# Five queue orders in a two-layer streaming encoder: sample bias sign, gate tiles, output weight loads, low-rank turns and sample rotary queries

## The chip, the cores and the metric

The kernel runs on one core of one Trainium2 chip. The metric is the device time of one launch in microseconds (us). Five engines of the core work side by side, each through its own list of instructions: PE does matmuls and transposes, DVE, ACT and POOL do elementwise work, and SP issues the DMA transfers. An engine waits where the next instruction of its list needs something that another engine, or a transfer, has not yet delivered.

## The reference, cut to what matters

The reference is one inference step of two transformer-like layers for 1024 prompt rows and 8 x 16 sample rows, the latter with caches of 512 earlier rows. Each layer projects x with one matrix and runs three groups of attention heads, each gated, whose results go through one output matrix and a layer norm:

```python
h = einsum('btd,de->bte', x, w_in)      # c_q, c_kv, k_rope, gates, fox q/k/v, log-forget, memory q
q   = _rms_norm(c_q, q_norm_g) @ w_uq;  q[..., 128:] = _rope(q[..., 128:], pos)
lat = _rms_norm(c_kv, kv_norm_g);       kr = _rope(k_rope, pos)
o_mla = _attend(q, [lat @ w_uk, kr], lat @ w_uv, chunk_causal=True)
o_fox = _attend(fq, fk, fv, logits += cq[t] - ck[s])   # cq, ck: running sums of log-forget
o_mem = softmax(mq @ mem_k) @ mem_v
mixed = concat([o_mla * silu(g_mla), o_fox * silu(g_fox), o_mem * silu(g_mem)])
y = layer_norm(ALPHA * x + mixed @ w_out)
```

All arithmetic is in float32 and the outputs also hold the new cache rows (latents, rotary keys, fox keys and values, log-forget).

## The kernel before, in words

A float32 product is made of three matmuls on operands split into a high and a low part (lines 192, 193 and 194: high by high, low by high or high by low). The split itself is a copy on ACT and a subtraction on DVE (L176, L177), and for weights a copy on ACT (L183) and a subtraction on POOL (L186). Work is tiled by 128 rows: tiles 0 to 7 are the prompt, tile 8 is all samples.

The two layers run the same stages one after the other, layer 0 up to about 755 us and layer 1 after it: memory gates (`w_ge`) and memory attention, with the fox gates (`w_gf`) and the sample memory attention woven in; forget sums and fox attention with its gates (`w_gm`); the low-rank projections; the queries, `qlat`, `qrope` and `s_qrope`; the latent (MLA) attention by head, with the sample attention woven in; and the output projection with the layer norm.

The order on each engine is not written by hand. The Python code emits the instructions through generators that are interleaved by small constants, and a scheduler with a timeline model then reorders them within their dependences and writes one list for each engine. Tiles come from pools with a fixed number of slots: a new tile waits until the readers of the slot's former tile are done. The pools that matter here are `w` (8 slots, weights and some large tiles), `u` (25 slots), `st` (4), `th` (3, shared by the tanh of the gates, by `o64` attention outputs that are stored to `md`, and by rotary temporaries named `rt`), and in PSUM `pss` (3), `psx` (2), `pst` (2) and `pso` (1).

The five places:

- **Sample bias sign** (`s_fox`, L1113, and `scores`, L1132 and L1134). The running forget sums of the sample rows are loaded into `scq` by four small DMAs, DVE multiplies them by -1 (L1113), and POOL later adds them to the key sums. The prompt's fox attention starts at the same time: ACT copies the transposed prompt sums to a tile `st`, SP stores it to DRAM (`ckd`), loads it back spread over all partitions (`ckb`, 512 KB), and POOL makes the bias tiles `pf` from it (L585, and L586 for the causal edge). DVE adds a score tile and its bias (L432). The queries `qf` are written by ACT and DVE (L351, L352).
- **Gate tiles** (`gates`, L374 and L376). ACT writes tanh(x/2) into a tile of the `th` pool, and DVE makes (tanh + 1) x from it into a tile of the `st` pool, which SP stores to `gd`.
- **Output weights** (`wout`). When head 3 of the MLA attention begins, all eight 512 KB row blocks of `w_out` are loaded (`raw`, from the `w` pool) and split into `woh` and `wol` in one piece of code.
- **Low-rank turns** (`lowrank`). Two passes go over the nine tiles, in the order 8, 0, 1, ... 7, the first with the weights `lr0` and the second with `lr1`, each 128 x 1224 in two halves. The second pass normalises each tile (`norm`; POOL scales the query part at L721) and rotates its key (`rope`, six DVE instructions L664 to L669, and a POOL copy at L725). After tile 0 the sample tile is transposed on PE, after tile 3 and after tile 7 four prompt tiles each (`turn`, through PE L201, then split). The tile `kr` comes from the `w` pool after the `lr1` weights.
- **Sample rotary queries** (`s_qrope`). One matmul, a rotation (`qturn`) and two transposes run in one go behind head 0 of the query projection.

## Time and profile before

| | us |
|---|---|
| median of 3 runs | 1462.06 (1461.39 to 1464.06) |
| the profiled execution, its own time | 1465.12 |
| its span | 1463.3 |
| PE busy | 1408.9 (96%) |
| DVE, ACT, POOL busy | 765.9, 617.5, 505.6 |

The page gives busy times and the chain of work that ended last. The view of waits lists, for one engine, what it waited for: the waiting group, the releasing group, the total in us, the number of waits, and the longest. The timeline lists instructions with start, duration and, in brackets, the idle time of the engine just before and what ended it. The windows view gives for a stretch the busy time and the number of instructions of each engine, and the clock that PE was granted (PEclk, 1.00 is full speed).

### The profile page before, as it was taken

How to read it: one execution, taken by the hardware profiler on the slowest of the kernel's cores; microseconds unless marked ns; L12 is line 12 of the kernel's file. 1: busy time of each engine (PE TensorE's matmuls, PEld its weight loads, DVE VectorE, ACT ScalarE, POOL GpSimd, SP SyncE). 2: the span in 40 equal slices, each digit the busy share in tenths (PEclk: the TensorE clock that was granted, in tenths of full speed). 3: DMA queues.
4: the chain of work that ended last, by engine and by line, in shares of the span. 5: the costliest groups of instructions: out<-in, count | busy, mean ns of one | idle time of the engine just before them, and what ended most of it. 6: DMA issues, size and time to landing. Idle time of an engine off the chain costs nothing.

```text
span 1463.3 us, 27842 instructions
## 1 busy us (share of the span) xinstructions
PE 1408.9 (96%) x10222; PEld 1262.3 (86%) x10222; DVE 765.9 (52%) x1961; ACT 617.5 (42%) x1624; POOL 505.6 (35%) x738
## 2 busy tenths in 40 slices
PE   7999999999999999999999999999999999998997
PEld 6998979988988788888899988899899887787886
DVE  6236445254345665656663374542633556556564
ACT  6345345355154444622233453543532544455100
POOL 0234145354263221611322242534534532235021
PEclk9999999999999999999999999999999999999999
DMA  7223332445354332363541234233543533433531
GB/s 281 90 76 94 118 104 82 127 128 152 94 169 132 120 115 77 115 220 101 183 167 54 85 98 146 69 95 111 160 135 112 171 114 113 125 116 119 172 127 72
DMA packets 142343, 180.63 MB, mean 123 GB/s; under 512 B 32384, under 2 KB 99776, under 8 KB 142208
## 3 DMA queue, kind: packets, MB, share of 16 engines
q1 hardware_dynamic: 142208, 178.86, 38.7%
q8 instruction: 81, 1.33, 0.4%
q14 instruction: 54, 0.44, 0.1%
HBM read 138.69 MB, written 40.12 MB: 122 GB/s over the span
## 4 chain that ended last, share of the span: by engine, by line
PE 80%; DMA 6%; DVE 5%; ACT 3%; POOL 2%; issue 2%; SPq 1%; POOLq 0%; DVEq 0%; ACTq 0%
PE pss L192 13%; PE pss L194 13%; PE pss L193 13%; PE pss L197 9%; PE pso L197 7%; PE pst L201 6%; PE psx L197 6%; PE psx L192 4%; PE psx L194 4%; PE psx L193 4%; SPq L164 1%; PE psx L201 1%; DMA scq<-cumd 1%; DMA raw<-in_w_out_dram 1%; DMA x<-in_x_t_dram 1%
## 5 line engine op out<-in xcount | busy, mean ns | idle before, releaser
L186 POOL TENSOR_TENSOR wl<-raw,wh 128x1024 fp32r<-128x1024 f32 (+3 forms) x40 | 101.5, 2541 | 232.5 <-ACT wh L183 124.1
L177 DVE TENSOR_TENSOR ptw<-pst,ptw 128x512 fp32r<-128x512 f32 (+1 forms) x192 | 121.8, 642 | 80.5 <-ACT ptw L176 78.2
L176 ACT CAST ptw<-pst 128x512 fp32r<-128x512 f32 (+1 forms) x192 | 103.1, 550 | 97.8 <-PE pst L201 78.2
L192 PE MATMUL psx<-xh,wh 128*128 128x256 f32 x384 | 110.6, 288 | 9.6 <-ACT wh L183 6.6
L192 PE MATMUL pss<-wh,xh 128*128 128x306 f32 (+1 forms) x384 | 118.4, 309 | 0.0
L193 PE MATMUL pss<-wl,xh 128*128 128x306 f32 (+1 forms) x384 | 117.8, 307 | 0.0
L194 PE MATMUL pss<-wh,xl 128*128 128x306 f32 (+1 forms) x384 | 117.5, 307 | 0.0
L192 PE MATMUL pss<-woh,msh 128*128 128x512 f32 x288 | 114.0, 396 | 0.5 <-ACT msh L1231 0.5
L194 PE MATMUL pss<-woh,msl 128*128 128x512 f32 x288 | 114.0, 397 | 0.1
L193 PE MATMUL pss<-wol,msh 128*128 128x512 f32 x288 | 113.5, 394 | 0.0
L192 PE MATMUL pss<-xh,wh 128*128 128x256 f32 x384 | 111.4, 290 | 0.0
L193 PE MATMUL psx<-xl,wh 128*128 128x256 f32 x384 | 109.6, 286 | 0.0
L193 PE MATMUL pss<-xl,wh 128*128 128x256 f32 x384 | 109.6, 285 | 0.0
L194 PE MATMUL pss<-xh,wl 128*128 128x256 f32 x384 | 109.4, 285 | 0.0
L194 PE MATMUL psx<-xh,wl 128*128 128x256 f32 x384 | 108.7, 284 | 0.0
L397 POOL TENSOR_SCALAR pa<-pa,col 128x128 f32<-128x128 f32 (+3 forms) x64 | 47.9, 757 | 139.5 <-DVE col L396 94.4
L192 PEld LDWEIGHTS psx<-xh,wh 128*128 128x128 f32 x384 | 73.9, 192 | 10.6 <-ACT wh L183 6.6
L197 PE MATMUL pso<-ptw,vh 128*128 128x256 f32 (+1 forms) x336 | 73.6, 295 | 5.8 <-ACT ptw L176 4.0
L192 PEld LDWEIGHTS pss<-wh,xh 128*128 128x128 f32 x384 | 72.4, 189 | 3.9 <-issue 2.9
L192 PEld LDWEIGHTS pss<-xh,wh 128*128 128x128 f32 x384 | 73.7, 192 | 1.5 <-DVE col L432 0.6
L420 ACT ACTIVATE pa<-pss,col 128x512 f32<-128x512 f32 (+3 forms) x96 | 55.4, 584 | 44.5 <-DVE col L418 27.5
L193 PEld LDWEIGHTS pss<-xl,wh 128*128 128x128 f32 x384 | 73.8, 192 | 0.3
(365 smaller groups left out, 4205.9 us busy)
## 6 DMA issues: line engine op xcount, KB each, us to landing
gd<-gg SPq DMA_DIRECT2D x64, 128.0 KB
kT<-in_fox_kt_dram SPq DMA_DIRECT2D x32, 256.0 KB
vraw<-in_fox_v_dram SPq DMA_DIRECT2D x32, 256.0 KB
kT<-in_mla_kt_dram SPq DMA_DIRECT2D x32, 256.0 KB
vraw<-in_mla_v_dram SPq DMA_DIRECT2D x32, 256.0 KB
raw<-in_w_out_dram SPq DMA_DIRECT2D x16, 512.0 KB
g<-md SPq DMA_DIRECT2D x16, 512.0 KB
raw<-in_w_lr_dram SPq DMA_DIRECT2D x8, 612.0 KB
```

Source lines behind the costliest of these rows:

```text
L164: self.nc.sync.dma_start(dst, src)
L176: nc.scalar.copy(hi, ps)
L177: nc.vector.tensor_tensor(lo, ps, self.f(hi), op=ALU.subtract)
L186: (self.nc.vector if dve else self.nc.gpsimd).tensor_tensor(lo, raw, self.f(hi), op=ALU.subtract)
L192: self.nc.tensor.matmul(ps, ah, bh, start=first and x == 0, stop=False)
L193: self.nc.tensor.matmul(ps, ah, bl, start=False, stop=False)
L194: self.nc.tensor.matmul(ps, al, bh, start=False, stop=last and x == n - 1)
L197: self.nc.tensor.matmul(ps, lhsT, rhs, start=start, stop=stop)
L201: self.nc.tensor.transpose(out, in_, self.ident[:k, :k])
L397: self.nc.gpsimd.tensor_scalar(p, p, rs, 1.0, op0=ALU.mult, op1=ALU.mult)
L420: nc.scalar.activation(p[:, a:b], pss[x][:, :b - a], AF.Exp, bias=nmx[:, one], accum_out=sm[:, x:x + 1])
```

## The change

It edits five places, in both layers.

1. The multiplication by -1 goes, and POOL subtracts `scq` where it added it.
2. The gates write tanh and product into the same `st` tile; no `th` tile is used.
3. `wout` becomes a generator of five steps that loads four, two and two blocks and splits the pairs a step later; it is stepped from the third step of head 2 on and at each step of head 3.
4. In `lowrank`, the keys of all nine tiles are rotated by six DVE instructions and one POOL copy after tile 3 of the first pass; `kr` is therefore taken from the `w` pool before the `lr1` weights. The turns of the sample tile and of tiles 0 to 3 come one tile later, and before the last turns stand two steps of `qlat`.
5. `s_qrope` yields between its rotation and its transposes, which now follow head 1.

```diff
-                t = self.th([P, 256])
-                nc.scalar.activation(t, ps, AF.Tanh, scale=0.5)
                 g = self.st([P, 256], name="gg")
-                nc.vector.scalar_tensor_tensor(g, t, 1.0, ps, op0=ALU.add, op1=ALU.mult)
+                nc.scalar.activation(g, ps, AF.Tanh, scale=0.5)
+                nc.vector.scalar_tensor_tensor(g, g, 1.0, ps, op0=ALU.add, op1=ALU.mult)
...
+            if i == 3:
+                kr = self.w([P, 9, 2, 64], name="kr")
+                x1, x2 = early[:, :, 32:64], early[:, :, 64:96]
+                t = self.pw([P, 2, 9, 32], name="rt")
+                k1, k2 = kr[:, :, 0, 0:32], kr[:, :, 0, 32:64]
+                nc.vector.tensor_tensor(t[:, 0], x2, self.sin, op=ALU.mult)
...
+                nc.gpsimd.tensor_copy(kr[:, :, 1, :], kr[:, :, 0, :])
         W = self.wprep(self.i["w_lr1"][l])
...
-        kr = self.w([P, 9, 2, 64], name="kr")
...
-            self.rope(kr[:, i, 0:1, :], early[:, i, 32:96].unsqueeze(1), i, 1, nc.vector)
-            nc.gpsimd.tensor_copy(kr[:, i, 1, :], kr[:, i, 0, :])
...
+            if i == 1:
+                turn8()
+                yield
+            if i == TURN[0] + 1:
+                turns(0)
+                yield
+        self.wq0 = self.wmla("w_uqn", l, 0, 3)
+        more()
+        turns(1)
+        yield
...
         q = self.qturn(ps, 8, self.st)
+        yield
         pt = self.pso() if QPO else self.pst()
...
-        nc.vector.tensor_scalar(cq, cq, -1.0, None, op0=ALU.mult)
...
-            nc.gpsimd.tensor_scalar(pr[:, 0:512], ck, 1.0, cq[:, p:p + 1], op0=ALU.mult, op1=ALU.add)
+            nc.gpsimd.tensor_scalar(pr[:, 0:512], ck, 1.0, cq[:, p:p + 1], op0=ALU.mult, op1=ALU.subtract)
...
-    def wout(self, l):
-        WO = []
-        for e in range(8):
-            raw = self.w([P, D], name="raw")
-            self.load(raw, self.i["w_out"][l, e * P:(e + 1) * P, :])
-            hi = self.u([P, D], F32R, "woh")
-            lo = self.u([P, D], F32R, "wol")
-            self.wsplit(hi, lo, raw)
-            WO.append((hi, lo))
-        return WO
+    def wout(self, l, WO):
+        raws = []
+        for step in range(5):
+            if step:
+                for raw in raws[2 * step - 2:2 * step]:
+                    hi = self.u([P, D], F32R, "woh")
+                    lo = self.u([P, D], F32R, "wol")
+                    self.wsplit(hi, lo, raw)
+                    WO.append((hi, lo))
+            for e in range(*((0, 4), (4, 6), (6, 8), (8, 8), (8, 8))[step]):
+                raw = self.w([P, D], name="raw")
+                self.load(raw, self.i["w_out"][l, e * P:(e + 1) * P, :])
+                raws.append(raw)
+            yield
...
-                if h == 3:
-                    WO.extend(self.wout(l))
+                    if h == 3 or h == 2 and x == 2:
+                        next(wo)
```

The scheduler sees other code, so all engines' lists shift, not only at the five places. Three places show it. Line numbers of the new kernel are one higher than those of the old one up to the rotation code, and others behind it.

**SP and DVE where fox attention starts in layer 0.** SP before; `ckd` is the store of the prompt sums, `ckb` their load, `md` stores of memory attention outputs:

```order
L164 DMA raw_3353<-in_w_kv_dram 128x1208 [waits Pool_49]
L167 DMA md_134<-th_2100 64x256 [waits DMAHW5_49,DVE_49]
L167 DMA gd_127<-gg_2132 128x256 [waits DMAHW6_49]
L167 DMA gtd_142<-ggt_2138 128x256 [waits DMAHW7_49,Activation_49]
L167 DMA gd_128<-gg_2168 128x256 [waits DMAHW0_49,DVE_49]
L167 DMA ckd_140<-st_2212 32x128 [waits DMAHW1_49,Activation_49]
L167 DMA cumd_141<-spr_2235 32x528 [waits DMAHW2_49]
L164 DMA raw_3355<-in_w_kv_dram 128x1208 [waits DMAHW3_49,Pool_49]
L164 DMA g_2733<-gd_127 64x256 [waits DMAHW6_49,DMAHW4_49]
L164 DMA ckb_2397<-ckd_140 128x1024 [waits DMAHW5_49,DMAHW1_49]
L164 DMA ckb_2842<-ckd_140 128x1024
```

The same place now:

```order
L168 DMA md_132<-th_2001 64x256 [waits DMAHW1_49,DVE_49]
L165 DMA g_2082<-gd_130 64x256 [waits DMAHW2_49]
L168 DMA gd_128<-gg_2149 128x256 [waits DMAHW3_49,DVE_49]
L168 DMA ckd_140<-st_2194 32x128 [waits DMAHW4_49,Activation_49]
L168 DMA cumd_141<-spr_2217 32x528 [waits DMAHW5_49]
L168 DMA md_133<-th_2064 64x256 [waits DMAHW6_49,DVE_49]
L165 DMA ckb_2379<-ckd_140 128x1024 [waits DMAHW7_49,DMAHW4_49]
L165 DMA g_2593<-gd_127 64x256 [waits DMAHW0_49]
L165 DMA kT_2463<-in_mem_kt_dram 128x512 [waits DMAHW1_49,PE_49]
L165 DMA vraw_2547<-in_mem_v_dram 128x512 [waits DMAHW2_49,PE_49]
L165 DMA ckb_2820<-ckd_140 128x1024 [waits DMAHW3_49]
L168 DMA md_134<-th_2084 64x256 [waits DVE_49]
```

The store of `ckd` and the first load of `ckb` now stand ahead of the last `md` store, which was ahead of them, and the second `ckb` load has left the first. On DVE the row of L1113 is gone. Before, DVE read:

```order
L352 SCALAR_TENSOR_TENSOR qf_2245<-pss_2334,qf_2245 64x256 [waits Activation_49]
L1113 TENSOR_SCALAR scq_4928<-scq_4928 128x4 [waits DMAHW2_49,DMAHW1_49,DMAHW7_49,DMAHW0_49,DVE_49]
L352 SCALAR_TENSOR_TENSOR qf_2246<-pss_2334,qf_2246 64x256 [waits Activation_49]
L432 ISA pf_2399,col_2410<-pss_2404,pf_2399 128x512 [waits PE_49,Pool_49]
L432 ISA col_2410 128x1
```

On PE the transpose of the prompt sums stands 113 rows ahead of the first fox score now, and stood 129 rows ahead before. Also on PE, in the stage before this one, the fox gates now lie in blocks between the transposes and value products of memory attention, where these products stood next to each other before and most gates after them.

**PE where the second low-rank pass starts in layer 0.** `wh` and `wl` are the split weights, `xsh` and `xh` the sample and prompt rows. Before, tile 7 of the first pass was followed by a whole half of the next weights:

```order
L193 MATMUL pss_5222<-wl_4840,xh_504 128x306
L194 MATMUL pss_5222<-wh_4839,xl_505 128x306
L192 MATMUL pss_5275<-wh_5262,xsh_572 128x306 [waits Activation_49]
L193 MATMUL pss_5275<-wl_5263,xsh_572 128x306 [waits Pool_49]
L194 MATMUL pss_5275<-wh_5262,xsl_573 128x306
L192 MATMUL pss_5275<-wh_5262,xsh_572 128x306
L193 MATMUL pss_5275<-wl_5263,xsh_572 128x306
```

Now the first matmul of three tiles comes first, and then the one that waits for POOL:

```order
L194 MATMUL pss_5194<-wl_4804,xh_500 128x306
L195 MATMUL pss_5194<-wh_4803,xl_501 128x306
L193 MATMUL pss_5246<-wh_5234,xsh_566 128x306 [waits Activation_49]
L193 MATMUL pss_5309<-wh_5234,xh_106 128x306 [waits Activation_49]
L193 MATMUL pss_5355<-wh_5234,xh_106 128x306 [waits Activation_49]
L194 MATMUL pss_5246<-wl_5235,xsh_566 128x306 [waits Pool_49]
L195 MATMUL pss_5246<-wh_5234,xsl_567 128x306
```

The low part `wl_5235` is written into a slot of the `w` pool that tile 7 of the first pass reads until 12 matmuls before its end; in the old list only the low part of the other half (`wl_5267`) had to wait for such a slot, and PE had 28 matmuls to do before it.

**ACT in the last head of the MLA attention, layer 0.** `woh` is the high part of an output weight block, `ptw` the high part of a transposed probability tile, `pa` the exponentials. Before:

```order
L183 CAST woh_7912<-raw_7910 128x1024 [waits DMAHW2_49]
L183 CAST woh_7918<-raw_7916 128x1024 [waits DMAHW4_49]
L183 CAST woh_7924<-raw_7922 128x1024 [waits DMAHW5_49,PE_49]
L176 CAST ptw_7859<-pst_7855 128x384 [waits PE_49,Activation_49]
L420 ACTIVATE pa_7829,col_7831<-pss_7816,col_7830 128x512 [waits DVE_49,Activation_49,Pool_49]
L420 ACTIVATE pa_7829,col_7831<-pss_7822,col_7830 128x512
L176 CAST ptw_7873<-pst_7868 128x512 [waits PE_49,Activation_49]
L183 CAST woh_7930<-raw_7928 128x1024 [waits DMAHW6_49]
```

Now:

```order
L184 CAST woh_8042<-raw_7822 128x1024 [waits DMAHW3_49]
L177 CAST ptw_7757<-pst_7753 128x384 [waits PE_49,Activation_49]
L177 CAST ptw_7771<-pst_7766 128x512 [waits DVE_49,PE_49]
L184 CAST woh_8046<-raw_7824 128x1024 [waits DMAHW4_49]
L419 ACTIVATE pa_7727,col_7729<-pss_7714,col_7728 128x512 [waits DVE_49,Pool_49]
L419 ACTIVATE pa_7727,col_7729<-pss_7720,col_7728 128x512
L419 ACTIVATE pa_7791,col_7793<-pss_7784,col_7792 128x128 [waits DVE_49,Activation_49,Pool_49]
L184 CAST woh_8156<-raw_7949 128x1024 [waits DMAHW6_49,PE_49]
L419 ACTIVATE pa_7806,col_7808<-pss_7799,col_7807 128x256 [waits DVE_49,Activation_49,Pool_49]
L184 CAST woh_8160<-raw_7951 128x1024 [waits DMAHW7_49,PE_49]
```

The casts of `woh` no longer stand three in a row ahead of a `ptw`; the seventh and eighth stand ahead of `pa` instead, and their `raw` loads are issued after the last score of head 2.

More of the change, by code (lines that the diff above doesn't have):

```diff
@@ L66 @@
 QLN = 1
+QLE = 2
 QLR = 4
@@ L364, in gates @@
                 self.tokproj(ps, X, 8, W, 256)
-                t = self.th([P, 256])
-                nc.scalar.activation(t, ps, AF.Tanh, scale=0.5)
                 gs = self.st([P, 256], name="ggs")
-                nc.vector.scalar_tensor_tensor(gs, t, 1.0, ps, op0=ALU.add, op1=ALU.mult)
+                nc.scalar.activation(gs, ps, AF.Tanh, scale=0.5)
+                nc.vector.scalar_tensor_tensor(gs, gs, 1.0, ps, op0=ALU.add, op1=ALU.mult)
                 yield
@@ L674, in rstd, with lowrank @@
         self.nc.gpsimd.tensor_tensor(ss, ss, self.mhalf, op=ALU.pow)
-    def lowrank(self, l, X):
+    def lowrank(self, l, X, more):
         nc = self.nc
@@ L695, in lowrank @@
             yield
+            if i == 3:
[4 more added lines that the diff above has]
+                nc.vector.tensor_tensor(t[:, 0], x2, self.sin, op=ALU.mult)
+                nc.vector.tensor_tensor(t[:, 1], x2, self.cos, op=ALU.mult)
+                nc.vector.tensor_tensor(k1, x1, self.cos, op=ALU.mult)
+                nc.vector.tensor_tensor(k2, x1, self.sin, op=ALU.mult)
+                nc.vector.tensor_tensor(k1, k1, t[:, 0], op=ALU.subtract)
+                nc.vector.tensor_tensor(k2, k2, t[:, 1], op=ALU.add)
+                nc.gpsimd.tensor_copy(kr[:, :, 1, :], kr[:, :, 0, :])
         W = self.wprep(self.i["w_lr1"][l])
@@ L767, in lowrank @@
                 self.split(LT[c][0][:, cs], LT[c][1][:, cs], turn(lt, tl))
-            self.split(KRH[:, cs], KRL[:, cs], turn(krs, tl))
+            self.split(KR[0][:, cs], KR[1][:, cs], turn(krs, tl))
             for a in range(2):
@@ L773, in lowrank @@
             self.store(o["p_kr"][l, 0, cs].rearrange("(a p) r -> p a r", p=P), kr[:, g * 4:g * 4 + 4, 0, :])
-            yield
-        self.lr = CQ, LT, (KRH, KRL)
+        KR = []
+        for n, i in enumerate(order):
+            ps = self.psw()
+            self.tokproj(ps, X, i, W, LRW)
+            norm(i, ps)
+            yield
+            if i == 1:
[8 more added lines that the diff above has]
+        yield
+        self.lr = CQ, LT, KR
     def qrope(self, l, CQ):
@@ L1200, in sample @@
         yield
[L1203 to L1212 removed]
+    def wout(self, l, WO):
[11 more added lines that the diff above has]
+                raws.append(raw)
+            yield
     def tail_start(self, l, xin):
@@ L1375, in step, with more @@
                 next(sg, None)
-        for x, _ in enumerate(self.lowrank(l, X)):
+        ql = self.qlat(l, self.qd[2][:, 0:2])
+        def more():
+            for _ in range(QLE):
+                next(ql)
+        for x, _ in enumerate(self.lowrank(l, X, more)):
             if x > 0:
@@ L1380, in layer @@
         CQ, LT, KR = self.lr
-        ql = self.qlat(l, self.qd[2][:, 0:2])
         Q = []
@@ L1385, in layer @@
             if h == 0:
-                self.s_qrope(l, self.qd[2][:, 2])
+                qr = self.s_qrope(l, self.qd[2][:, 2])
+            if h < 2:
+                next(qr)
             for _ in range(QLN if h else 0):
@@ L1401, in layer @@
         WO, start, ready = [], [], []
+        wo = self.wout(l, WO)
         def mlau():
```

41 lines of the change are left out of this document (14 added, 27 removed).

## Prediction

> **What bounds the kernel now.** I read the page first: how busy each engine is and what the last chain consists of.
>
> ```profile
> span 1463.3 us, 27842 instructions
> PE 1408.9 (96%) x10222; PEld 1262.3 (86%) x10222; DVE 765.9 (52%) x1961; ACT 617.5 (42%) x1624; POOL 505.6 (35%) x738
> PE 80%; DMA 6%; DVE 5%; ACT 3%; POOL 2%; issue 2%; SPq 1%; POOLq 0%; DVEq 0%; ACTq 0%
> ```
>
> PE is busy for 1408.9 of 1463.3 us. The change removes no matmul that counts, so it can only win from the 54 us in which PE does nothing, and from stretches in which PE's clock is low. Work taken from DVE, ACT or POOL (52%, 42%, 35%) counts only where PE waits for it. So the second view is what PE waits for (group that waits, group that releases, us in all, times, longest); a wait that no line names can give nothing back.
>
> ```profile
> PE psx L192 <- ACT wh L183: 7.2, 2, 6.6
> PE pss L197 <- DVE qf L352: 6.0, 2, 3.3
> PE pst L201 <- POOL h L721: 4.9, 4, 1.4
> PE pso L197 <- ACT ptw L176: 4.5, 6, 1.9
> PE pst L201 <- DVE qrt L669: 2.6, 2, 1.3
> PE pso L197 <- DVE th L486: 2.1, 4, 0.6
> PE pso L197 <- DVE ptw L177: 2.0, 8, 0.3
> PE pst L201 <- DVE fkl L570: 2.0, 2, 1.1
> PE pss L197 <- ACT pa L420: 1.7, 4, 0.5
> ```
>
> The first is the program's start, which the change leaves alone; L669 belongs to `qrope`, left alone too. The rest are the places of the change: `qf` (bias sign), `h` L721 (low-rank turns), `ptw` and `pa` (partly output weights), and `th`, `fkl`, `ptw` L177 (memory attention, where the gates run). The sample rotary queries appear in no line. The third view, windows, shows PE's idle time in these stages and the granted clock (columns: window, length, then busy time of PE, PEld, DVE, ACT and POOL, then PEclk).
>
> ```profile
> 130.00:142.00 12.00, 8.49 (x62) 6.98 (x60) 10.19 (x31) 7.21 (x23) 5.04 (x15) 1.00 0.25 60
> 186.00:191.50 5.50, 1.98 (x15) 1.08 (x13) 2.37 (x8) 1.40 (x4) 4.99 (x8) 0.98 0.44 145
> 191.50:194.60 3.10, 3.10 (x15) 3.06 (x15) 1.41 (x7) 2.38 (x6) 3.10 (x4) 0.50 0.25 87
> 383.70:386.70 3.00, 3.00 (x23) 2.95 (x21) 0.00 (x0) 0.27 (x1) 0.00 (x0) 1.00 0.00 0
> 601.00:604.30 3.30, 3.30 (x15) 3.30 (x15) 1.56 (x5) 1.15 (x5) 3.30 (x3) 0.50 0.00 0
> 855.00:866.00 11.00, 8.15 (x60) 6.84 (x60) 9.80 (x30) 6.78 (x22) 5.00 (x15) 1.00 0.28 71
> 915.30:918.50 3.20, 3.20 (x16) 3.20 (x16) 1.36 (x7) 2.36 (x6) 3.20 (x4) 0.53 0.22 82
> 1324.00:1327.00 3.00, 3.00 (x22) 2.88 (x22) 2.12 (x8) 1.60 (x5) 3.00 (x2) 1.00 0.05 16
> ```
>
> After the `qf` waits PE runs for 3.1 and 3.2 us at a clock of 0.50 and 0.53, and after layer 0's output weight stall for 3.3 us at 0.50. The same stall in layer 1 is followed by 1.00. A stall thus can cost a second time: half of 3.1, of 3.3 and 0.47 of 3.2, about 1.5 us each.
>
> The prices come from one profiled execution of 1465.12 us, 3.1 over the median of 1462.06. I take the sum of differences from the median.
>
> **Bias sign.** Before, this happens in layer 0:
>
> ```profile
> L649 ACT COPY st<-pst x1: 265/265/265, 172.4 to 172.4; 32x128 f32<-32x128 f32 x1
> 174.65 0.46 SPq L167 DMA_DIRECT2D md<-th  x1
> 176.85 0.38 SPq L167 DMA_DIRECT2D ckd<-st  x1
> 179.28 0.88 SPq L164 DMA_DIRECT2D ckb<-ckd  x2
> 186.51 4.34 POOL L585 TENSOR_SCALAR pf<-ckb,ncq 128x640 f32<-128x640 f32 x5 [12.18 <-DMA ckb<-ckd]
> 188.67 0.54 DVE L1113 TENSOR_SCALAR scq<-scq 128x4 f32<-128x4 f32 x1 [4.99 <-DMA scq<-cumd]
> 189.82 0.30 PE L197 MATMUL pss<-fkh,qf 128*128 128x128 f32 x1 [3.29 <-DVE qf L352]
> 190.46 0.50 PE L197 MATMUL pss<-fkh,qf 128*128 128x512 f32 x1 [0.23 <-DVE col L432]
> 190.81 1.28 POOL L586 TENSOR_SCALAR_AFFINE_SELECT pf<-pf 128x128 f32<-128x128 f32 x5
> ```
>
> DVE stands at L1113 until the four `scq` loads land, with the second `qf` queued behind it, and PE waits 3.29 us, then 0.23. L1113 goes. But what is late next? The score tiles are freed by DVE's L432, which needs POOL's bias: the five L585 run from 186.51 and the first of five L586 ends near 190.81 + 1.28 / 5 = 191.1, and the matmuls of the next gate wait for that, starting near 191.5. Had `ckb` landed at the same moment, PE would have its first scores earlier and would wait for the bias until the same 191.5: the edit alone would bring nothing. So its worth is how much earlier `ckb` lands. ACT had the sums ready at 172.4 + 0.27 = 172.7, and SP issued the store at 176.85, held up by `md` at 174.65: 4.1 us late. The new SP order has the store and the first `ckb` ahead of that `md`. Against it, the transpose of the sums stands 113 rows ahead of the first score instead of 129; 16 rows at 0.13 us (23 matmuls in 3.00 us, windows) are 2.1 us. So `ckb` comes between 2.0 and 4.1 us earlier; I take 2.8 of the 3.5 us in layer 0, and 2.6 of the 6.0 - 3.3 + 0.2 = 2.9 us in layer 1, whose chain is the same: -5.4. A rest of 0.7 us is too short to bring the low clock, if the 1.9 us stall of layer 1 above is a measure: -3.0 more. Together **-8.4**, between 0 (`ckb` as late as now) and -9.4 (all gone).
>
> [...]
>
> **Gate tiles.** ACT had waited for a `th` slot that an `md` store held:
>
> ```profile
>   DMA md<-th: 2.5, 2
> ```
>
> That goes (2.5 us of ACT, twice in all), and with fewer users of `th` the scheduler puts gate matmuls between the steps of memory attention. There PE is idle for 12.00 - 8.49 = 3.5 us (130 to 142) and 11.00 - 8.15 = 2.9 us (855 to 866), in waits of up to 0.3 to 0.6 us for splits and outputs that nothing covers (`ptw` L177 and `th` above). Blocks of gate matmuls cover that. I take half of 6.4, since only part of the small waits has a block beside it: **-3.0**. Bounds: -6.4, and +2.5, if ACT now waits as long for a `st` slot held by a `gd` store, with the exponentials queued behind it.
>
> **Low-rank turns and key rotation.** All four waits for L721 (4.9 us) should go:
>
> ```profile
> 437.30 1.00 POOL L186 TENSOR_TENSOR wqk<-raw,wqk 128x384 fp32r<-128x384 f32 x1 [0.64 <-ACT wqk L183]
> 438.40 0.58 POOL L721 TENSOR_SCALAR h<-h,col 128x384 f32<-128x384 f32 x1
> ```
>
> Here POOL splits a `qlat` weight for 1.00 us ahead of the scaling that PE needs; now the scaling stands first, and PE has two `qlat` steps ahead of the turn. The sample's turn gains a whole tile, 24 matmuls of 0.13 us or 3.1 us, against waits of 4.9 / 4 = 1.2. But `kr` now takes a slot of the `w` pool early, and the low part of the first `lr1` half must wait for tile 7 of the first pass:
>
> ```profile
> 357.98 2.80 POOL L186 TENSOR_TENSOR wl<-raw,wh 128x1224 fp32r<-128x1224 f32 x1 [2.03 <-ACT wh L183]
> 389.79 2.83 POOL L186 TENSOR_TENSOR wl<-raw,wh 128x1224 fp32r<-128x1224 f32 x1 [29.00 <-PE pss L193]
> ```
>
> It takes 2.83 us, as at 389.79. PE has 12 matmuls of tile 7 and three first matmuls to cover it, 15 x 0.13 = 2.0 us; a new wait of 0.8 to 0.9 us per layer, +1.7. Together **-3.2**; bounds -4.9 (covered) and +0.8 (2 x 2.83 uncovered). The second half follows behind 36 more matmuls, 4.7 us, and is covered.
>
> ```profile
> L666 DVE TENSOR_TENSOR kr<-early,cos 128x32 f32<-128x32 f32 x9 | 2.7, 302 | 1.2 <-PE pss L193 1.2
> ```
>
> Of rotations, 54 small DVE instructions like these (0.20 to 0.30 us) become 6 of 288 columns. DVE's other work hides both; I take 0, up to +1 if the batch stands in front of a split.
>
> **Output weights.** In layer 0:
>
> ```profile
> 597.14 1.05 ACT L183 CAST woh<-raw 128x1024 fp32r<-128x1024 f32 x1 [1.83 <-DMA raw<-in_w_out_dram]
> 598.10 0.47 ACT L176 CAST ptw<-pst 128x384 fp32r<-128x384 f32 x1
> 598.62 0.38 PE L197 MATMUL pso<-ptw,vh 128*128 128x256 f32 x1 [1.61 <-ACT ptw L176]
> ```
>
> ACT waits 1.83 us for a `raw` to land and casts it for 1.05 us, with `ptw` queued behind. PE waits 1.61 us here and up to 1.9 in layer 1, and with the small waits behind (`pa` 0.5) about 2.5 in each layer, 5.0, plus 1.6 for the low clock in layer 0. In the new order `ptw` is free of it, but the seventh and eighth cast stand ahead of `pa`, and their loads are issued after head 2's last score, so ACT will wait again: I estimate 1.5 to 2.5 us per layer from the 1.83 + 1.05 above less some cover, 3.8. That is -1.2, and half of the 1.6 for the clock: **-2.0**, from -6.6 (no wait) to +3.3 (1.6 more clock loss in each layer).
>
> **Sample rotary queries.** No wait of PE names it, so 0; its weight load now comes after the `lr1` weights are free, at worst two waits like L669's: +2.6.
>
> **New waits.** All lists are reordered, also where nothing was edited. I add **+2.5**, one pair of waits like L669's (2.6).
>
> Sum: -8.4 - 3.0 - 3.2 - 2.0 + 2.5 = -14.1; 1462.1 - 14.1 = **1448.0 us**.
>
> **The rivals.**
>
> - *The bias takes `scq`'s place.* `ckb` lands no earlier, and PE's wait moves to the gate behind the scores. For it: L585 waited 12.18 us for `ckb`, and the sums are transposed later. Against it: SP's order. Seen as PE waiting for L431's result near POOL's mask; -8.4 is lost: 1456.4.
> [...]
> - *All gates and weights are covered.* No new waits, nothing for `lr1`, the memory stage without idle time: -2.5 - 1.7 - 3.4 more: 1440.4.
> - *Nothing is left.* Each freed wait is met by the next one: about 1461, no change.
> - *Slower: the `w` pool is a slot short.* With `kr` in it, the `lr1` load itself, not just the split, waits for tile 7. A load, `ckb`, took up to 186.51 - 179.28 = 7.2 us; with a cast of 1.05 and the split of 2.83, 11.1 us, less 2.0 of cover, and 1.5 for the clock: 10.6 per layer, 21.2 in place of 1.7: 1467.5. It decides from 8 us per layer on. Against it: in the new SP order both loads are released by a matmul of the stage before.
>
> **How the numbers follow.** A measurement of this kernel can tell about 0.2%, 2.9 us, from no change. My forecast gets 0.43, the bias 0.20, the clock 0.10, full cover 0.10, nothing left 0.08, slower 0.09. Faster: 0.83; same 0.08; slower 0.09. The range takes in the first four: 1440 to 1458 (the 1456.4 and half of the +2.6). It leaves out no change, slower, and a bit below.
>
> **What would show it.** Right: no PE wait for `qf`; clock 1.00 behind the first fox scores; L585 starting ahead of PE's first fox score; no wait for the scaled `h`; a wait of about 0.9 us for `wl` at the start of the second pass; a wait for `pa` behind `woh` late in the MLA attention; PE idle for about 1.7 and 1.5 us in the memory stage. Wrong: a PE wait of 3 us at the first fox gate with POOL's L585 just before it; a wait of several us on the `lr1` weights; clocks of 0.5 where no wait is.

## The result and the profile after

The changed kernel takes 1439.82 us (median of 4 runs, 1437.29 to 1441.50) against 1463.06 for the kernel before beside it. The ratio is 0.9833 with a 95% interval of 0.9813 to 0.9853: 1.7% or some 24 us faster. In a later run, `after_again`, it was 1440.91 and 0.9799 (0.9772 to 0.9826). The prediction said 1448.0 and a range from 1440 to 1458: the sign was right, and the gain was 10 us larger than the sum, which put the time just below the range.

The page of the changed kernel, its span and PE's line:

```profile
span 1437.9 us, 27746 instructions
PE 1402.4 (98%) x10222; PEld 1257.8 (87%) x10222; DVE 756.6 (53%) x1863; ACT 620.8 (43%) x1624; POOL 515.8 (36%) x722
```

PE's idle time within the span went from 54 to 35.5 us, and its busy time fell by 6.5 us with the same 10222 instructions. What PE waits for now:

```profile
PE psx L193 <- ACT wh L184: 7.3, 2, 6.7
PE pst L202 <- DVE fkl L569: 2.3, 2, 1.4
PE pso L198 <- ACT ptw L177: 2.2, 6, 0.6
PE pso L198 <- DVE ptw L178: 2.0, 8, 0.3
...
PE pss L198 <- ACT pa L419: 1.1, 4, 0.4
...
PE pss L194 <- POOL wl L187: 0.5, 2, 0.3
```

Behind the program's start nothing over 2.3 us is left. The lines for `qf` (6.0), `h` (4.9), `th` (2.1) and `qrope`'s `qrt` (2.6) are gone, the last of which no part of the prediction had touched. The new wait for `wl` is there, at 0.5 us in both layers together instead of the 1.7 that I had put in.

By stages, from the starts of their first matmuls in the two timelines (us):

| stage | layer 0 before, after | layer 1 before, after |
|---|---|---|
| start to the first memory product, or from the output projection on | 96.7, 97.3 | 193.6, 194.2 |
| memory stage, to the first fox score | 88.5, 87.0 | 87.6, 85.5 |
| fox attention, to the first low-rank matmul | 170.7, 163.0 | 169.8, 163.3 |
| low-rank and queries, to the first MLA tail matmul (`xnh`) | 134.5, 133.8 | 134.4, 133.7 |
| MLA attention, to the output projection | 138.0, 132.8 | 136.5, 133.2 |

The output projection of layer 1 to the last matmul takes 104.9 and 104.8, and the span's end 8.2 and 9.3. Fox attention gives 14.2 us of the 25.4 between the two spans, MLA attention 8.5, the memory stage 3.6. The third and fourth row belong together, since 20 PE instructions of the sample attention moved from the MLA stage to the queries: 9.9 us in all.

The place where fox attention starts in layer 0, in the timeline of the changed kernel:

```profile
172.25 1.44 SPq L168 DMA_DIRECT2D ckd<-st  x1
174.25 0.46 SPq L168 DMA_DIRECT2D md<-th  x1
175.04 0.34 SPq L165 DMA_DIRECT2D ckb<-ckd  x1
179.33 4.35 POOL L584 TENSOR_SCALAR pf<-ckb,ncq 128x640 f32<-128x640 f32 x5 [8.74 <-DMA ckb<-ckd]
184.33 0.45 PE L198 MATMUL pss<-fkh,qf 128*128 128x512 f32 x1
```

The sums are stored ahead of the `md` store, and `ckb` is there 5.0 us ahead of PE's first score; before, it came 1.2 us behind it (POOL started on it at 186.51):

```profile
185.28 0.45 PE L197 MATMUL pss<-fkh,qf 128*128 128x512 f32 x1
```

The windows of the changed kernel, with the clock in the third column from the right:

```profile
186.00:190.00 4.00, 4.00 (x31) 3.83 (x32) 1.96 (x10) 3.73 (x9) 4.00 (x4) 1.00 0.68 229
135.00:138.00 3.00, 3.00 (x14) 3.00 (x15) 2.75 (x7) 2.66 (x12) 1.89 (x7) 0.50 0.20 9
128.00:140.00 12.00, 9.99 (x70) 9.35 (x69) 10.94 (x31) 5.53 (x18) 6.06 (x16) 0.86 0.32 89
839.00:851.00 12.00, 10.36 (x84) 9.52 (x83) 10.91 (x32) 6.44 (x21) 5.29 (x16) 1.00 0.35 107
```

PE is fully busy at full clock behind the scores. The memory stage is idle for 2.0 and 1.6 us, about as forecast; but layer 0 has a new stretch of half clock at 135 to 138 us (0.50), which it did not have before.

### The profile page after: what moved, and what is told of

Same layout as the page of the kernel before. It is cut to its first block, busy times and chain, and to the rows that moved or that the text cites. A ratio compares the mean times of both kernels' runs of the same rounds, so it can differ in the third digit from the quotient of the medians.

```text
span 1437.9 us, 27746 instructions
## 1 busy us (share of the span) xinstructions
PE 1402.4 (98%) x10222; PEld 1257.8 (87%) x10222; DVE 756.6 (53%) x1863; ACT 620.8 (43%) x1624; POOL 515.8 (36%) x722
## 4 chain that ended last, share of the span: by engine, by line
PE 87%; DMA 4%; DVE 3%; ACT 2%; POOL 2%; issue 1%; SPq 0%; POOLq 0%; DVEq 0%; ACTq 0%
PE pss L193 15%; PE pss L195 14%; PE pss L194 14%; PE pss L198 10%; PE pso L198 7%; PE pst L202 7%; PE psx L198 6%; PE psx L193 4%; PE psx L195 4%; PE psx L194 4%; DMA memx<-in_mem_t_dram 1%; POOL wl L187 1%; PE psx L202 1%; DMA raw<-in_w_uqn_dram 1%; DMA g<-md 1%
## 5 line engine op out<-in xcount | busy, mean ns | idle before, releaser
L177 ACT CAST ptw<-pst 128x512 fp32r<-128x512 f32 (+1 forms) x192 | 103.4, 552 | 97.3 <-PE pst L202 88.9
L184 ACT CAST wh<-raw 128x1024 fp32r<-128x1024 f32 (+4 forms) x52 | 54.8, 1057 | 45.7 <-PE pss L194 14.4
L195 PEld LDWEIGHTS pss<-wh,xl 128*128 128x128 f32 x384 | 72.3, 189 | 1.6 <-issue 1.6
```

Source lines behind the costliest of these rows:

```text
L177: nc.scalar.copy(hi, ps)
L184: self.nc.scalar.copy(hi, raw)
L195: self.nc.tensor.matmul(ps, al, bh, start=False, stop=last and x == n - 1)
```

## The experiments

All ratios are to the kernel before, run beside them on the same chip, with 95% intervals. Four of the five edits were run alone (the turns together with the two `qlat` steps), three were undone, and a few runs move one thing only.

| run | median us | ratio |
|---|---|---|
| only_scq | 1463.94 | 0.9974 (0.9958 to 0.9990) |
| only_gates | 1452.35 | 0.9891 (0.9861 to 0.9921) |
| only_turns | 1460.64 | 0.9945 (0.9925 to 0.9965) |
| only_wout | 1466.97 | 0.9993 (0.9977 to 1.0009) |
| only_qlat | 1461.38 | 0.9961 (0.9948 to 0.9975) |
| undo_scq | 1447.95 | 0.9894 (0.9869 to 0.9919) |
| undo_gates | 1459.94 | 0.9970 (0.9955 to 0.9985) |
| undo_wout | 1439.29 | 0.9829 (0.9805 to 0.9853) |
| qle0 | 1444.62 | 0.9864 (0.9838 to 0.9891) |
| th_four | 1461.95 | 0.9974 (0.9961 to 0.9988) |
| tanh_xst | 1472.51 | 1.0047 (1.0029 to 1.0064) |
| tanh_st | 1436.62 | 0.9796 (0.9777 to 0.9815) |
| ckb_on_act | 1454.31 | 0.9891 (0.9865 to 0.9917) |
| after_again | 1440.91 | 0.9799 (0.9772 to 0.9826) |
| tanh_st_again | 1436.63 | 0.9774 (0.9744 to 0.9804) |

The runs form four sets, each beside its own executions of the kernel before: only_scq, only_gates, only_turns and only_wout (before 1468.87); undo_scq, undo_gates, undo_wout and qle0 (1464.69); only_qlat, th_four, tanh_xst and tanh_st (1466.51); ckb_on_act and the last two (1469.98). The kernel before thus differs by 5 us between sets, and a difference between runs of two sets is uncertain by about as much.

**only_scq: the bias sign alone.**

```diff
-        nc.vector.tensor_scalar(cq, cq, -1.0, None, op0=ALU.mult)
...
-            nc.gpsimd.tensor_scalar(pr[:, 0:512], ck, 1.0, cq[:, p:p + 1], op0=ALU.mult, op1=ALU.add)
+            nc.gpsimd.tensor_scalar(pr[:, 0:512], ck, 1.0, cq[:, p:p + 1], op0=ALU.mult, op1=ALU.subtract)
...
```

> Before with the bias sign edit alone; the lists of SP and PE around the place stay as they were. Theory (the prediction's step): the wait of 3.3 and 2.7 us for qf goes, but the bias tiles come as late as before, since ckb lands no earlier, so PE waits about as long at the first gate matmul behind the scores: 0 to -1 us, half clock behind it as before. Rival: the edit itself is worth its wait, -6.0 for the waits and up to -3 for the clock, -6 to -9 us.

Measured: -0.26% (0.10 to 0.42), about 4 us. Its waits of PE, and a row of its timeline:

```profile
PE pss L192 <- DVE col L432: 4.0, 2, 2.4
PE pss L197 <- DVE col L432: 3.4, 4, 1.7
```

```profile
192.80 0.38 PE L192 MATMUL pss<-xh,wh 128*128 128x256 f32 x1 [2.38 <-DVE col L432]
```

The line for `qf` is gone, and in its place PE waits for DVE's L432, which needs POOL's bias: 0.66 and 2.38 us in layer 0, 1.70 and 1.59 in layer 1, 6.3 us where there were 6.5. The wait merely moved, as the theory said. The 4 us were somewhat more than the 0 to 1 expected; with the profile's waits nearly equal I can't place them.

**only_gates: the gate tiles alone.**

```diff
-                t = self.th([P, 256])
-                nc.scalar.activation(t, ps, AF.Tanh, scale=0.5)
                 g = self.st([P, 256], name="gg")
-                nc.vector.scalar_tensor_tensor(g, t, 1.0, ps, op0=ALU.add, op1=ALU.mult)
+                nc.scalar.activation(g, ps, AF.Tanh, scale=0.5)
+                nc.vector.scalar_tensor_tensor(g, g, 1.0, ps, op0=ALU.add, op1=ALU.mult)
...
```

> Before with the gate tiles alone. Theory: the list of SP is what the gate tiles change, so the store of the sums and ckb come earlier, and with them the scq loads that are queued behind; the idle time of the memory stage shrinks by about 3 us in all and the wait for qf shrinks although the negation stays: -3 to -9 us. Rival: the gate tiles bring only the memory stage, and the wait for qf stays at 3.3 and 2.7: -2 to -4 us.

Measured: -1.09% (0.79 to 1.39), about 16 us, above both. In the profile the wait for the second `qf` is as long as ever:

```profile
PE pss L197 <- DVE qf L352: 7.0, 2, 3.5
PE pst L201 <- POOL h L719: 5.2, 4, 1.5
```

and `ckb` is there 4.7 and 5.5 us ahead of the first score, so L1113 alone still holds the place shut when the bias is early. The memory stage is 2.7 and 2.3 us shorter. That does not make 16, but the profiled execution took 1460.09 us and was the slowest of six (from 1447.01 on): it shows a run in which the edit gave little. Part of what the quicker ones saved is the clock: a mean of 0.991 over a span of 1458.3 us loses 13.1 us, and 0.997 over the quickest span of 1445.2 us loses 4.3, so the clock makes some 9 of the 13 us between these two. The rest is not seen.

**only_turns: later turns, key rotation in one batch, and two qlat steps ahead.** The edit is the `lowrank` part of the diff above, with `QLE = 2`.

> Before with the low-rank turns, the batched key rotation and the two earlier qlat steps alone. Theory: the four waits for the scaled h (4.9 us) go and 0.5 us come back at the start of the second pass: -4 to -5 us; the wait for qrope's rotation (2.6 us in two) stays. Rival: the 2.6 us belong to this edit too, because the qlat steps that are taken ahead leave other work for qrope: -6.5 to -7.5 us.

Measured: -0.55% (0.35 to 0.75), about 8 us. No wait for `h` and none for `qrt` is left, so the rival holds: the two belong together. The wait for `ptw` in the MLA attention is also gone, although `wout` is the old one: that stage is 133.3 and 133.2 us long, as in the changed kernel, with the same 20 PE instructions moved out of it.

**only_wout: the output weights in steps alone.** The edit is the `wout` part of the diff.

> Before with the output weight loads in steps alone. Theory (the prediction's step): a new wait for pa behind the seventh and eighth cast takes back most of it, -1 to -2 us. Rival: the loads of these blocks land before ACT reaches their casts, so the waits go whole: -4 us, and -1.6 for the half clock of layer 0, -4 to -6 us.

Measured: -0.07% (-0.09 to 0.23), nothing that can be told from zero. The wait stays, a little shorter:

```profile
PE pst L201 <- POOL h L721: 4.9, 4, 1.3
PE pso L197 <- ACT ptw L176: 3.0, 6, 1.1
```

Here ACT still has two `woh` casts and a third that waits for its load in front of a `ptw`. The loads' steps do not take the casts from ahead of it.

**undo_wout: the changed kernel with the output weights in one piece.**

```diff
...
+                if h == 3:
+                    WO.extend(self.wout(l))
...
-                    if h == 3 or h == 2 and x == 2:
-                        next(wo)
```

> The changed kernel with the output weights loaded and split in one piece again. Theory: the stall before ptw was ended by another edit, which moved the slots of the w pool and with them ACT's list, not by the steps: within 1.5 us of the changed kernel. Rival (the prediction): the steps take the casts from ahead of ptw, so 2 to 6 us come back.

Measured: 1439.29 us and 0.9829, the changed kernel's time. PE's list is the changed kernel's, row by row. With only_wout this shows that the edit has no part in the gain; the new order of ACT's list, which I had read as its effect, comes from elsewhere.

**qle0: without the two qlat steps ahead.**

```diff
-QLE = 2
+QLE = 0
```

> The changed kernel without the two qlat steps ahead of the last turns (they come later, as before). ACT's list then has three woh casts in a row ahead of a ptw again. Theory: these two steps carry qrope's wait (2.6 us in two) and, through the w pool, the output weight stall (2 to 4.5 us in two, 1.7 more if the half clock follows): +5 to +8 us against the changed kernel, and the waits for the scaled h of the last turn may come back by up to 2.5. Rival: the later turns alone do it, and nothing but the h waits of up to 2.5 us comes back.

Measured: 1444.62 us, 0.9864 where the changed kernel has 0.9833 and 0.9829 (undo_wout, same chip): about 5 us.

```profile
PE pso L198 <- ACT ptw L177: 3.2, 8, 0.8
PE pst L202 <- DVE qrt L668: 2.6, 2, 1.3
```

`qrope`'s 2.6 us are back whole. The MLA attention is 2.6 and 2.0 us longer, but the 20 PE instructions are back in it, and the stage before it is 0.8 and 0.3 us shorter, so the two together lose 3.5 us. The stall in front of `ptw` is not back as it was: 3.2 us with 0.8 at most, where the kernel before had 4.5 with 1.9. The waits for `h` do not come back, so the later turns ended those.

**only_qlat: before, with nothing but these two steps ahead.**

```diff
+QLE = 2
...
                 self.wq0 = self.wmla("w_uqn", l, 0, 3)
+                more()
...
+        def more():
+            for _ in range(QLE):
+                next(ql)
...
```

> Before with nothing but two qlat steps taken ahead of the last low-rank turns. Theory: these steps alone carry the wait for qrope's rotation (2.6 us in two), cover the last turn's wait for h (about 2.5 of the 4.9), and put ptw ahead of the waiting woh casts (about 4 us of waits, 1.7 for the half clock of layer 0): -8 to -11 us against before. Rival: key rotation and later turns are needed as well, since kr's slot moves the w pool; then only qrope's 2.6 goes: -2 to -4 us.

Measured: -0.39% (0.25 to 0.52), some 6 us, between both.

```profile
PE pss L198 <- DVE qf L353: 4.9, 2, 2.8
PE pst L202 <- POOL h L722: 2.4, 2, 1.2
```

No `qrt`, no `ptw` of that size, and only two of the four waits for `h`. MLA attention takes 133.6 and 133.1 us, the stage before it 136.6 and 135.5, 2.1 and 1.1 more than before, since 20 PE instructions moved; the two together give 4.6 us. Two `qlat` steps taken earlier thus end `qrope`'s wait, half of those for `h`, and the output weight stall. They are enough for the stall, but with the other edits in place it is mostly gone without them too (qle0).

**undo_scq: the changed kernel with the negation put back.**

```diff
+        nc.vector.tensor_scalar(cq, cq, -1.0, None, op0=ALU.mult)
...
-            nc.gpsimd.tensor_scalar(pr[:, 0:512], ck, 1.0, cq[:, p:p + 1], op0=ALU.mult, op1=ALU.subtract)
+            nc.gpsimd.tensor_scalar(pr[:, 0:512], ck, 1.0, cq[:, p:p + 1], op0=ALU.mult, op1=ALU.add)
...
```

> The changed kernel with the multiplication by -1 put back (POOL adds again). SP still has ckb early. Theory: with the bias early, the loads of scq are what is late, and DVE stands at the multiplication with the second qf behind it until about 187 us, 2.5 us past the point where PE needs it: waits of about 2.5 to 3 us for qf in each layer and up to 3.4 us for the half clock, so +5 to +9 us against the changed kernel. Rival: the edit is worth only what it was worth alone, where the wait merely moved: +0 to +3 us.

Measured: 1447.95 us, 8 above the changed kernel.

```profile
PE pso L198 <- DVE th L485: 5.4, 2, 2.7
PE pss L198 <- DVE qf L353: 4.1, 2, 3.5
```

The `qf` wait is there again with 3.5 us in layer 0 (0.6 in layer 1), but a wait of 2.7 us for `th` in each layer is new, some 12 us into the low-rank stage (at 365.40 and 1080.44 us), where nothing was edited: the new lists brought that. In the profile, the slowest execution of six, fox attention is 6.3 and 0.8 us longer than in the changed kernel and the low-rank stage 3.8 and 5.3; the clock is 0.54 from 368 to 370 us and 0.50 from 1080 to 1082. So the size fits the theory, and less than half of it comes by the mechanism named.

**undo_gates: the changed kernel with the gate tiles as before.** The diff of only_gates, backwards.

> The changed kernel with the separate tanh tiles put back; SP's list has ckb behind the last md store again. Theory: the memory stage loses its blocks of gate matmuls, +3 of waits and about +2 in shorter losses, and the bias is late again, so PE waits at the first fox gate as it does with the bias sign edit alone, about 6 us in both layers, and up to 3.4 for the clock: +11 to +14 us. Rival: the bias edit does not need the gate tiles, so only the memory stage comes back: +3 to +6 us.

Measured: 1459.94 us and 0.9970, 20 us above the changed kernel.

```profile
PE pss L193 <- DVE col L433: 4.7, 2, 2.4
PE pss L198 <- DVE col L433: 3.4, 4, 1.2
```

PE waits for the bias as in only_scq (1.0 of the 3.4 us are two waits later in fox attention, which the changed kernel has too). Fox attention is 171.5 and 172.6 us long (163.0 and 163.3 in the changed kernel), the memory stage 88.5 and 87.8. The direction is the theory's, the size is 6 us more.

**ckb_on_act: the same, with the sums' transfers on another list.**

```diff
-        self.store(self.ckd.rearrange("h (i t) -> (h i) t", t=P), s)
+        self.nc.scalar.dma_start(self.ckd.rearrange("h (i t) -> (h i) t", t=P), s)
...
-        self.load(t, self.ckd[h:h + 1, :].partition_broadcast(P))
+        self.nc.scalar.dma_start(t, self.ckd[h:h + 1, :].partition_broadcast(P))
```

> The changed kernel with the gate tiles as before, but the store and the loads of the prompt sums (ckd, ckb) issued from ACT's list right behind the copy, not from SP's; PE's list is the one of the kernel with the gate tiles undone. Theory: there the bias was late because SP stood on md stores; from ACT it comes 4 us earlier and the waits of 3.6 and 3.5 us at the first fox scores and gate go, with up to 3.4 for the half clock: -6 to -10 us against the kernel with the gate tiles undone. Rival: the bias is late for another reason (the sums are made late, or the loads are slow), and the waits stay: 0 to -2 us.

Measured: 1454.31 us where undo_gates had 1459.94, 5.6 us less. The ratios, 0.9891 and 0.9970, would give 11.5, but the kernel before was 5 us slower in this set; against the changed kernel of its own set undo_gates is 20.7 us slower and this run 13.4, which gives 7.3. So the gain is 6 to 11 us. PE's list is that of undo_gates but for three instructions in each layer, which stand a few places off behind the first scores.

```profile
PE pso L198 <- DVE th L487: 2.1, 4, 0.6
...
PE pss L193 <- DVE col L433: 1.3, 1, 1.3
...
PE pss L198 <- DVE col L433: 1.0, 2, 0.5
```

Of the 7.1 us of waits for the bias at the start of fox attention 1.3 are left, the later 1.0 stays, and no stretch of half clock lies between 40 us and the end (the mean clock is 0.996). Fox attention is 9.5 us shorter in all. This is the cleanest of the runs: the bias was late because SP's list had its transfers behind stores that were not ready. Against PE's first score `ckb` is there 2.4 and 4.8 us earlier, of which 1.5 and 2.6 are the earlier issue; the rest is a quicker load (6.2 and 4.8 us, where undo_gates has 7.2 and 7.0), which the edit may have brought by the other list or by what was loaded beside it.

**th_four: the gate tiles as before, with a fourth `th` slot.**

```diff
-TH_BUFS = 3
+TH_BUFS = 4
...
-        return self.sp.tile([P, w], F32, tag=f"xcol{w}", bufs=4, name=self.nm(name))
+        return self.sp.tile([P, w], F32, tag=f"xcol{w}", bufs=3, name=self.nm(name))
...
```

> The changed kernel with the gate tiles as before, and four th slots instead of three (the xcol pools have three slots instead of four to make room). Theory: it is not the number of th slots; the lists of PE and SP at the place are those with three, so it is as slow as with the gate tiles undone: +17 to +22 us against the changed kernel. Rival (the prediction): a gate's tanh waits for a th slot that an md store holds, and a fourth slot ends that: 0 to +8 us.

Measured: 1461.95 us and 0.9974, as slow as with three slots. ACT's waits for a `th` slot that an `md` store holds are gone (2.3 us in undo_gates, none here), so the rival, which was the prediction's reason, falls.

```profile
PE pss L193 <- DVE col L433: 4.4, 3, 2.4
PE pss L198 <- DVE col L433: 3.0, 4, 1.5
```

**tanh_xst: the tanh in a tile of another pool (`xst`), not in place.**

```diff
...
+                t = self.xst([P, 256])
+                nc.scalar.activation(t, ps, AF.Tanh, scale=0.5)
                 g = self.st([P, 256], name="gg")
-                nc.scalar.activation(g, ps, AF.Tanh, scale=0.5)
-                nc.vector.scalar_tensor_tensor(g, g, 1.0, ps, op0=ALU.add, op1=ALU.mult)
+                nc.vector.scalar_tensor_tensor(g, t, 1.0, ps, op0=ALU.add, op1=ALU.mult)
...
```

> The changed kernel with the tanh of the gates in a tile of the xst pool instead of in place; memory attention and gates interleave on PE, but SP's list has the md stores and the scq loads ahead of ckb. Theory: the memory stage stays as short as changed, but the bias is late and PE waits for it at the first fox scores or the first fox gate, 5 to 8 us in both layers with up to 3.4 for the half clock: +6 to +11 us against the changed kernel. Rival: the place of ckb in SP's list does not matter, and the interleaving is all: within 2 us.

Measured: 1472.51 us, 0.5% slower than before and over 30 us slower than the changed kernel; no theory had that. Its waits, and two windows:

```profile
PE pso L198 <- DVE th L487: 8.3, 6, 2.8
PE pss L198 <- DMA lnw<-lsd: 6.3, 2, 3.2
PE pss L198 <- DVE lf L630: 5.4, 2, 2.7
```

```profile
164.00:190.00 26.00, 15.45 (x81) 12.54 (x80) 10.64 (x28) 4.95 (x14) 4.76 (x11) 0.61 0.45 123
892.00:914.00 22.00, 11.27 (x52) 8.92 (x53) 9.26 (x26) 3.66 (x12) 4.27 (x10) 0.69 0.54 145
```

PE waits for the outputs of memory attention, for the forget gates and for a small load, and PE's clock is 0.61 and 0.69 over more than 20 us: the gates had all been used up earlier, and the end of memory attention and the forget sums stood alone. The memory stage is 101.7 and 101.3 us long. There is no wait for the bias here, since PE came later itself, so the run says nothing on `ckb`. It shows that the gates work as cover by where they lie, and that moving them can lose more than the change gained.

**tanh_st: the tanh in an `st` tile of its own.**

```diff
...
+                t = self.st([P, 256])
+                nc.scalar.activation(t, ps, AF.Tanh, scale=0.5)
                 g = self.st([P, 256], name="gg")
-                nc.scalar.activation(g, ps, AF.Tanh, scale=0.5)
-                nc.vector.scalar_tensor_tensor(g, g, 1.0, ps, op0=ALU.add, op1=ALU.mult)
+                nc.vector.scalar_tensor_tensor(g, t, 1.0, ps, op0=ALU.add, op1=ALU.mult)
...
```

> The changed kernel with the tanh in one st tile and the product in another, so not in place, but out of the th pool; SP's list has ckb ahead of the last md stores as in the changed kernel. Theory: it is leaving the th pool that counts: within 2 us of the changed kernel. Rival: in place counts, because two st tiles for each gate leave ACT waiting for gd stores: +3 us or more.

Measured: 1436.62 us, 3 below the changed kernel's first median, so writing in place is not what counts. I ran it again beside the changed kernel.

> The changed kernel, beside the next one on one chip: 1438 to 1442 us by the runs so far, 0.983 of before.

> The changed kernel with the tanh in an st tile of its own and the product in another. Theory: the gates' place in PE's list is the same but for small shifts, so it is within 2 us of the changed kernel; what looked like 4 us less was the half clock windows, of which its profile had two fewer. Rival: it is faster for good, by 3 to 6 us.

Measured: 1440.91 (1437.69 to 1441.90) and 1436.63 (1435.69 to 1438.10). The ranges hardly touch: it is 4 us faster for good, the fastest of all, and my expectation of no difference was wrong. About 1.1 us of it is the end of the program (9.3 us behind the last matmul, 8.2 here). By their mean clocks (0.997 of 1438.1 us, 0.995 of 1436.3) the changed kernel's profile lost some 4 us to the low clock and this one's some 7, so that is not it. The rest stays open.

## Why the predicted gain was too small, point by point

The terms of the sum against the two profiles (PE's waits of 0.1 us and more, and 1.7 us for each stretch of half clock):

| term | forecast | found |
|---|---|---|
| bias sign | -8.4 | -9.9 (waits -6.5, clock -3.4) |
| gate tiles | -3.0 | -3.6 (the whole stage) |
| low-rank turns | -3.2 | -4.4 |
| output weights | -2.0 | -5.6 (waits of MLA attention -3.9, clock -1.7) |
| `qrope` | 0 | -2.6 |
| other waits, not in the sum | 0 | -3.2 |
| new waits | +2.5 | +2.5 |

That is 26.8 us, and the stages outside the edits are 2.2 us longer; together 24.6 of the 25.4 us between the spans. It is not as close stage by stage: fox attention gave 3 us more than its waits and clock, and the stages from low-rank to MLA attention 2.5 less. Three steps of the prediction failed. It held that the last casts of the output weights would make ACT wait for their loads again, 3.8 us; no such wait came, and the stall went by another edit than the one it was booked to. It put at nothing waits that no edit touched but that the new lists ended, `qrope`'s (2.6) and small ones (3.2). And it took the bias sign 1.5 us too small and gave the negation alone what needs the gate tiles as well.

**Bias sign (-8.4).** Right in mechanism: the negation alone moves the wait (only_scq), the bias is what is late next, and its place in the issuing list decides most of it (ckb_on_act). The size came short: all 6.5 us of waits went, not 5.4, since `ckb` came 6.2 us earlier against the first score in layer 0 and not 2.0 to 4.1. The term that I left out is the load itself: it took 179.33 - 175.04 = 4.3 us instead of 7.2. A second `ckb` was issued 0.5 us behind the first before and 2.3 us behind it now, but that is not what counts. In tanh_xst the second stands 0.4 us behind, and POOL starts on the first after 4.2 us:

```profile
190.33 0.88 SPq L165 DMA_DIRECT2D ckb<-ckd  x2
194.52 4.35 POOL L586 TENSOR_SCALAR pf<-ckb,ncq 128x640 f32<-128x640 f32 x5 [18.16 <-DMA ckb<-ckd]
```

The slow load had a weight load issued just ahead of it, 1.15 us in the kernel before:

```profile
178.13 0.36 SPq L164 DMA_DIRECT2D raw<-in_w_kv_dram  x1
```

In layer 1 before, such a load stood 1.0 us ahead and POOL started on the first `ckb` 6.4 us after its issue. In the changed kernel the last such load stood 7.2 and 6.4 us ahead, and `ckb` took 4.3 us in layer 0 and at most 4.0 in layer 1. No run moved that load alone.

Both stretches of half clock behind the scores went too. Fox attention gave 14.2; beyond the waits at its start and the clock (9.9) lie waits for `th` of 0.4 in each layer and for the sample's `spr` of 0.9 and 0.4, which ended without being forecast (against a new one of 0.6 for `ptw` in each layer), and some 3 us spread over many instructions.

**Gate tiles (-3.0).** The memory stage gave 3.6, near the term. The step that failed is the reason and the reach. A fourth `th` slot does nothing (th_four), while a tile of `st`, in place or not, does (tanh_st), and a tile of `xst` ruins the order (tanh_xst): it is the list that the scheduler makes of it, not the shortage of slots. And I booked the earlier `ckb` to the bias sign, where it needs the gate tiles: undone, 20 us of the 24 go. Neither edit gets it alone: with the bias sign alone PE waits for POOL, with the gate tiles alone for `qf`. Alone they measured 4 and 16 us, and undone 8 and 20, so the terms can't be added.

**Low-rank turns (-3.2).** Right in mechanism, 1.2 us too small: the four waits for `h` went, and the `lr1` weights brought 0.5 us instead of 1.7.

**Output weights (-2.0).** The effect was larger and the cause wrong. I had read ACT's new list and put it down to the steps of `wout`; undo_wout and only_wout show that these do nothing, and only_qlat that the two `qlat` steps are enough. The new wait for `pa` that I estimated at 3.8 us did not come: ACT reaches the last two casts without idle time before them.

```profile
588.71 1.05 ACT L184 CAST woh<-raw 128x1024 fp32r<-128x1024 f32 x1
...
590.10 1.05 ACT L184 CAST woh<-raw 128x1024 fp32r<-128x1024 f32 x1
```

The loads, issued from 584.94 us on, had landed when ACT got to these casts, with the softmax work ahead of them. MLA attention gave 5.2 and 3.3 us, part of it by the 20 PE instructions that moved.

**Sample rotary queries and `qrope` (0).** I had written that L669's wait is left alone. It went, by 2.6 us, with the `qlat` steps (qle0 brings it back). The split of `s_qrope` itself was not tried alone.

**New waits (+2.5).** Right in the total, by luck: no pair of that size came, but small new waits in both layers (`ptw` in fox attention 0.6 each, `h` 0.2, `cqh` 0.3 and 0.2, `qn` 0.2) add up to 2.5 us. In undo_scq the new lists brought 5.4 in one pair, and in tanh_xst more. Such a term is a guess on a draw, and belongs in the range.

Of the rivals, the bias in `scq`'s place is what only_scq is; full cover (1440.4) was the nearest, and had been given 0.10. The lower bound of 1440 stood on it and left no room for waits that end without an edit of theirs.

**The clock.** Behind the former stalls it is at 1.00, as said: in the changed kernel from 138.21 to 1431.80 us without a break. Before has five stretches of half clock beside the end of the program (0.50 for 3.41 us each, at 17.2, 34.3, 191.3, 600.9 and 914.9 us) and the changed kernel two, one of them of double length (at 32.4 and 134.8 us); each 3.41 us of them lose 1.7. Here are the 3.41 us of the kernel before ahead of the last three, with PE's busy time behind the length, and then three windows of the same length that no half clock followed. All six are laid whole multiples of 3.413 us behind the first stretch.

```profile
187.87:191.28 3.41, 1.23 (x7) 0.99 (x7) 2.15 (x6) 0.51 (x2) 3.41 (x6) 1.00 0.50 165
597.47:600.88 3.41, 1.96 (x14) 1.77 (x15) 1.54 (x7) 3.41 (x8) 3.41 (x2) 1.00 0.22 75
911.50:914.91 3.41, 1.11 (x6) 0.87 (x7) 2.04 (x6) 0.38 (x2) 3.41 (x6) 1.00 0.62 192
129.83:133.25 3.42, 2.18 (x18) 1.74 (x16) 2.93 (x14) 0.53 (x2) 0.73 (x2) 1.00 0.41 129
133.25:136.66 3.41, 2.75 (x20) 2.35 (x21) 3.00 (x8) 3.36 (x13) 2.45 (x10) 1.00 0.20 8
1321.09:1324.50 3.41, 2.15 (x15) 1.96 (x16) 1.75 (x7) 3.41 (x8) 3.41 (x2) 1.00 0.22 76
```

And the window ahead of the new stretch in the changed kernel:

```profile
131.39:134.80 3.41, 1.58 (x10) 1.04 (x9) 2.92 (x12) 1.18 (x4) 1.17 (x4) 1.00 0.08 31
```

PE was busy for 1.23, 1.96, 1.11 and 1.58 us of 3.41 ahead of half clock, and for 2.18, 2.75 and 2.15 us where none followed. The length of a stall does not sort them: half clock followed the 1.6 us stall of layer 0 (1.96 us busy) and not the 1.9 us stall of layer 1 (2.15). And waits of 1.4, 0.2 and 0.3 us in the memory stage, which lie in one of these windows now (1.58), were followed by the new stretch at 135 us, where the similar waits before, from 1.1 us down, lay in two (2.18 and 2.75) and were followed by none. The busy time alone does not sort them either, if the window is laid elsewhere: with PE busy for less than in three of the four windows ahead of half clock, the one around layer 1's stall was followed by 1.00.

```profile
1319.50:1322.91 3.41, 1.21 (x9) 0.87 (x8) 1.10 (x5) 2.34 (x5) 3.41 (x3) 1.00 0.53 177
1322.91:1326.32 3.41, 3.41 (x28) 3.38 (x29) 2.33 (x9) 2.69 (x8) 3.41 (x2) 1.00 0.12 38
```

What decides it is not shown, since no run moved a stall in time or changed its length alone. The prediction gave 0.10 to a clock that stays low though the stalls go; that did not come.

## What to carry to other kernels

Taking away an instruction that an engine waits in pays only if the next operand is there; look for what the released engine needs next, and for the list that issues its transfer. When several edits go through a scheduler, a list's row shows that something moved but not which edit moved it: make the edits one at a time before a row is booked to one. And a wait for data that is ready can be a store in front of it on the issuing engine: moving the store of the sums and its loads to another list gave 6 to 11 us. Half clock did not come by the length of a wait here (behind 1.6 us in layer 0, not behind 1.9 us in layer 1): price it from the clock that the trace shows, place by place, and not from the wait.

## What the runs showed of the hardware

A 512 KB broadcast load landed after 7.2 us where a weight load had been issued 1.15 us ahead of it (before, layer 0), and after 4.2 us without one, with a second broadcast load 0.4 us behind (tanh_xst). No run moved the weight load alone, so that it is the cause is not shown. Half clock (0.50) came in stretches of 3.41 us in the kernel before, of 6.83 and 3.41 us in the changed kernel, and of up to 20.5 us in tanh_xst; each 3.41 us of it lose 1.7. In the 3.41 us ahead of four of these stretches PE was busy for 1.11 to 1.96 us; what decides is not shown. Half clock differs between executions of one kernel: the changed kernel has a stretch at 135 us and after_again has none there (1.00 from 128 to 140 us), and runs of only_gates had a mean clock from 0.991 to 0.997 and spans from 1458.3 to 1445.2 us with it. A difference under 5 us thus needs several executions, not one profile.
